# Joined edits on a one-core transformer chain: GpSimd out of most splits and of the state-space mixer, 512-column products with a fold

## The chip, the cores and the metric

The kernel runs on one NeuronCore of a Trainium2 chip. The metric is the device time of one execution in microseconds. Five engines work side by side, each through its own instructions in their order: TensorE (PE, with its weight loads as PEld), VectorE (DVE), ScalarE (ACT), GpSimd (POOL) and SyncE (SP, which here only issues DMAs).

## The reference

A chain of two blocks over one sequence of 256 tokens with 1024 features, all in fp32:

```python
def first_block(x, ...):
    for layer in range(2):
        h = rms_norm(x, norm_mix[layer])
        if layer < 1:
            x = x + s5_mixer(h, ...)                       # state-space mixer, gated output
        else:
            x = x + stick_breaking_attention(h, w_q, k_shared, v_shared, w_o)
        x = x + conv_ffn(rms_norm(x, norm_ffn[layer]), w_up, conv_w, conv_b, w_down)
        if layer == 0:
            kv = rms_norm(x, norm_kv) @ kv_w               # shared keys and values
    return rms_norm(x, norm_final)

def second_block(x, ...):
    for i in range(2):
        x = layernorm(DN_ALPHA * x + 0.5 * swiglu(x, w13[i, 0], w2[i, 0]), ...)
        y = hybrid_mixer(x, ...)    # w_in: windows' q, k, v; conv'd qkv; z; gates
        x = layernorm(DN_ALPHA * x + y, ...)
        x = layernorm(DN_ALPHA * x + 0.5 * swiglu(x, w13[i, 1], w2[i, 1]), ...)
    return x

def s5_mixer(h, ...):
    u = h @ w_in        # then 64 groups of 16 channels, 64 complex states each
    ...                 # bu = u * B, scan with ab = exp(a dt), y = Re(C s) + d u
    z = gelu(y) @ w_glu
    return z[..., :1024] * sigmoid(z[..., 1024:])

def hybrid_mixer(x, ...):
    ...                 # ya: sliding windows of 128, yb: gated delta rule, chunks of 64
    return (sigmoid(gate_a) * (ya @ w_branch_a) + sigmoid(gate_b) * (yb @ w_branch_b)) @ w_out
```

The inner width of the feed-forward networks (FFNs) is 2816; there are two with a convolution of width 3 before the SiLU and four without.

## The kernel before, in words

**Products.** TensorE multiplies in the type fp32r, and each operand is held as a high and a low half: `split` (L146) lets ScalarE cast the operand to its high half (L150) and VectorE subtract that from it for the low half (L154). Its argument `share` gives the last columns of the subtraction to GpSimd. `mm3` (L183) makes one product of three matmuls: high times low, high times high, low times high. `unit` (L158) loads 128 x 1024 weights (512 KB) through the SP queue (L161) into `raw` and splits them into `wh` and `wl`. `cols_steps` (L199) multiplies a unit with the activations: 8 k-tiles of 128 features, each `mm3` over 256 columns, the tokens, all in one PSUM half bank. `toks` and `rows` are the products whose stationary operand is the activations; their matmuls have 256 and 512 columns.

**Order.** TensorE's order is fixed by `weave`, which takes steps from generators by a clock of its own; the other engines' instructions are put in order by the scheduler of the framework. `ahead` loads and splits the first units of the next stage early.

**Stages.** The state-space mixer `ssm` makes, for each of 8 `kt`, `u = w_in h` (`inputs`, unit split with `SH_I` = 384 columns on GpSimd), then builds 128-row matrices from the powers of the decay: `gt` from `Z` and `b`, `ca` from `W` and `c` (`group`), each a complex product: a VectorE multiply, a GpSimd multiply into `prod`, and an add (L770), which is GpSimd's for `ca` from the second `kt` on. The powers in `W` are made by GpSimd too (`step`). Then come scans on VectorE (L819) and 16- to 32-column products. `Glu` follows, with units split with `SH_Y` = 640 columns on GpSimd. In `ffn` (L405) step m of 22 multiplies the gate and the up unit into the two halves of one PSUM bank; `gate` reads the gate half from PSUM (ScalarE's SiLU, L386, or the convolution, L396 to L401), VectorE multiplies with the up half (L423), the result is split (`gh`, `gl`), and the down product of step m - `LAG` (7) follows, accumulated in four banks of the eight. `stick_breaking` has keys, queries and values of the same form; `hybrid` has the windows' keys and queries (`plain`), convolved channels (`conv`, `SH_C`), `z`, gates and branches (`SH_G`, `SH_B`, `SH_Z` = 640). The branches end in sums `keep`, and w_out is a `row_gemm` over 8 units, of which the last MH = 5 go to the hold pools, opened before the spare pool at the end of the kernel's `build`.

Of the kernel before, what the change touches and what calls it, by code (L numbers as in the profile page):

```python
# [12 lines left out]
ALU = mybir.AluOpType  # L13
# [77 lines left out]
class Core:  # L91
# [114 lines left out]

    def toks(self, out, ws, x, t):
# [14 lines left out]
    def ahead(self, x, srcs):  # L222
# [161 lines left out]
    def silu_gate(self, pool, ps, m):  # L384
        s = pool.tile([P, T], F32, name="s")
        self.nc.scalar.activation(out=s, in_=ps[:, 0, :], func=AF.Silu)  # L386
        return s

    def conv_gate(self, cw, cb):
# [3 lines left out]
        def gate(pool, ps, m):  # L393
            g = ps[:, 0, :]
# [11 lines left out]
    def ffn(self, x, state, up, down, gate, tail, after):  # L406
# [5 lines left out]
        with ExitStack() as ctx:  # L412
# [7 lines left out]
            def gated(m, ps):  # L420
                s = gate(act, ps, m)
                p = act.tile([P, T], F32, name="p")
                nc.vector.tensor_tensor(out=p, in0=s, in1=ps[:, 1, :], op=ALU.mult)  # L423
# [11 lines left out]
            def turn():  # L435
                yield "first"
                yield HOP
                for m in range(2):
# [34 lines left out]
SHARE = 512  # L473
# [27 lines left out]
def ssm(c, yT, after):  # L501
# [27 lines left out]
    with ExitStack() as ctx:  # L529
# [27 lines left out]
        with ExitStack() as prep:  # L557
# [111 lines left out]
            def step(R, src, dst, n, l, e=V):  # L669
# [3 lines left out]
                tt(ta, R[:, :, src], l[:, None, 0:1].to_broadcast(sh_), ALU.mult, e)  # L673
                tt(tb, R[:, ::-1, src], l[:, 1:3, None].to_broadcast(sh_), ALU.mult, e)
                tt(R[:, :, dst], ta, tb, ALU.add, e)
# [47 lines left out]
        hx = c.ktiles(hT)  # L723
# [30 lines left out]
        def group(kt):  # L754
# [7 lines left out]
            for R, n, x, y, pool, name in ((Z, TS, "b_re", "b_im", q3, "gt"), (W, TS + 1, "c_re", "c_im", cq, "ca")):  # L762
# [6 lines left out]
                tt(p, f(1), h(y), ALU.mult, G)  # L769
# [1097 lines left out]
```

## Time and profile before

| what | us |
| --- | --- |
| median of three runs (2253.45 to 2261.68) | 2254.35 |
| the profiled execution | 2259.23 |
| its span in the trace | 2257.5 |
| TensorE busy (95%) | 2146.6 |
| weight loads busy (87%) | 1968.0 |
| VectorE busy (65%) | 1466.2 |
| ScalarE busy (49%) | 1102.8 |
| GpSimd busy (23%) | 510.7 |

The span runs from the first to the last instruction in the trace; the execution's time is 1.7 us longer. A matmul's record lasts longer than its share of the engine, since matmuls overlap: the pace of TensorE is read from the distance of the starts. Along the span the stages are: state-space mixer to about 166 us, Glu to 250, convolution FFN to 440, attention to 580, two FFNs to 950, hybrid mixer to 1305, two FFNs to 1690, hybrid mixer to 2052, the last FFN to the end.

### The profile page before, as it was taken

Reading aid. Unit: us, or ns where it says so; the run is one execution under the profiler, and the core shown is the slowest. Engines: PE = TensorE matmul, PEld = TensorE weight load, DVE = VectorE, ACT = ScalarE, POOL = GpSimd, SP = SyncE. Lnnn points to the kernel's source line nnn. Section 1 sums busy time; section 2 is a strip of 40 time slices with the busy share of each in tenths; the row PEclk is TensorE's granted clock in tenths of the full one; section 3 lists DMA queues with packets and bytes.
Section 4 is the critical chain, followed back from the end, with each engine's and each line's share of the span. In section 5 each row is a group of like instructions: output and inputs, shape, how many; then the busy total and the mean of one; then the engine's idle time right before and its main releaser. Section 6 shows DMA issues by size and latency. Waiting matters only on the chain.

```text
span 2257.5 us, 40264 instructions
## 1 busy us (share of the span) xinstructions
PE 2146.6 (95%) x15892; PEld 1968.0 (87%) x15892; DVE 1466.2 (65%) x2352; ACT 1102.8 (49%) x1951; POOL 510.7 (23%) x519
## 2 busy tenths in 40 slices
PE   5679999999999999998999899999999899999998
PEld 5568999888999999897889899989989788998997
DVE  8974766676666555689754765565558886466555
ACT  4344554454545544466555444444445656543442
POOL 7542100101000100252534410020015344342000
PEclk8779999999999999999999999999999999999999
DMA  4214576544556556554443655556565454264663
GB/s 153 66 34 149 167 240 188 173 138 140 177 185 197 183 185 187 165 170 145 133 118 121 207 157 186 185 183 197 186 188 157 133 154 122 92 203 154 194 188 121
DMA packets 123486, 362.27 MB, mean 160 GB/s; under 512 B 24732, under 2 KB 38000, under 8 KB 123296
## 3 DMA queue, kind: packets, MB, share of 16 engines
q1 hardware_dynamic: 117696, 350.25, 49.7%
q0 software_dynamic: 5232, 9.37, 1.5%
q8 instruction: 125, 2.05, 0.4%
q14 instruction: 65, 0.53, 0.1%
q10 hardware_dynamic: 368, 0.07, 0.0%
HBM read 355.36 MB, written 5.04 MB: 160 GB/s over the span
## 4 chain that ended last, share of the span: by engine, by line
PE 75%; DVE 10%; DMA 5%; issue 5%; ACT 2%; POOL 1%; ACTq 0%; POOLq 0%; DVEq 0%
PE ps L36 72%; PE ps L40 3%; DVE wl L154 3%; DMA raw<-in_ffn_w_dram 2%; ACT wh L150 2%; DMA raw<-in_w_in_z_dram 1%; DVE xl L154 1%; DMA k<-scratch 1%; DVE keep L1053 1%; DVE k L1053 1%; DVE ea L513 0%; POOL u L1052 0%; DVE keep L1052 0%; DMA raw<-in_w_out_dram 0%; DVE er L709 0%
## 5 line engine op out<-in xcount | busy, mean ns | idle before, releaser
L154 DVE TENSOR_TENSOR wl<-raw,wh 128x1024 fp32r<-128x1024 f32 (+3 forms) x622 | 718.3, 1158 | 543.4 <-ACT wh L150 541.2
L150 ACT CAST wh<-raw 128x1024 fp32r<-128x1024 f32 x622 | 649.4, 1049 | 659.4 <-PE ps L36 344.2
L36 PE MATMUL ps<-xl,wh 128*128 128x256 f32 x3056 | 880.4, 288 | 8.5 <-DVE xl L154 6.2
L36 PE MATMUL ps<-xh,wh 128*128 128x256 f32 x3056 | 866.1, 283 | 0.0
L36 PE MATMUL ps<-xh,wl 128*128 128x256 f32 x3056 | 865.9, 283 | 0.0
L36 PEld LDWEIGHTS ps<-xl,wh 128*128 128x128 f32 x3056 | 587.9, 192 | 32.8 <-issue 19.1
L36 PEld LDWEIGHTS ps<-xh,wh 128*128 128x128 f32 x3056 | 587.2, 192 | 3.9
L36 PEld LDWEIGHTS ps<-xh,wl 128*128 128x128 f32 x3056 | 586.8, 192 | 0.0
L154 POOL TENSOR_TENSOR wl<-raw,wh 128x512 fp32r<-128x512 f32 (+2 forms) x172 | 293.3, 1709 | 1183.9 <-ACT wh L150 1126.7
L36 PE MATMUL ps<-wl,gh 128*128 128x512 f32 x528 | 208.9, 396 | 0.0
L36 PE MATMUL ps<-wh,gl 128*128 128x512 f32 x528 | 208.3, 394 | 0.5 <-DVE gl L154 0.5
L36 PE MATMUL ps<-wh,gh 128*128 128x512 f32 x528 | 208.0, 394 | 0.0
L36 PE MATMUL ps<-wl,xh 128*128 128x256 f32 (+1 forms) x576 | 188.2, 327 | 11.8 <-DVE wl L154 11.8
L36 PE MATMUL ps<-wh,xl 128*128 128x256 f32 (+1 forms) x576 | 183.1, 318 | 0.8 <-DVE xl L154 0.7
L36 PE MATMUL ps<-wh,xh 128*128 128x256 f32 (+1 forms) x576 | 182.4, 317 | 0.0
L36 PEld LDWEIGHTS ps<-wl,xh 128*128 128x128 f32 x576 | 110.7, 192 | 21.4 <-DVE wl L154 12.7
L36 PEld LDWEIGHTS ps<-wh,gl 128*128 128x128 f32 x528 | 99.2, 188 | 24.3 <-DVE gl L154 1.3
L36 PEld LDWEIGHTS ps<-wh,xl 128*128 128x128 f32 x576 | 110.8, 192 | 9.9 <-DVE xl L154 2.7
L36 PEld LDWEIGHTS ps<-wh,xh 128*128 128x128 f32 x576 | 111.0, 193 | 6.5
L36 PEld LDWEIGHTS ps<-wl,gh 128*128 128x128 f32 x528 | 99.7, 189 | 18.8
L36 PEld LDWEIGHTS ps<-wh,gh 128*128 128x128 f32 x528 | 99.2, 188 | 18.5
L150 ACT CAST xh<-ps 128x512 fp32r<-128x512 f32 (+1 forms) x68 | 34.0, 517 | 115.5 <-PE ps L40 113.3
(286 smaller groups left out, 2446.8 us busy)
## 6 DMA issues: line engine op xcount, KB each, us to landing
raw<-in_ffn_w_dram SPq DMA_DIRECT2D x264, 512.0 KB, 4.3
raw<-in_ffn_w_up_dram SPq DMA_DIRECT2D x88, 512.0 KB, 4.1
raw<-in_w_in_qkv_dram SPq DMA_DIRECT2D x48, 512.0 KB, 4.1
raw<-in_ffn_w_down_dram SPq DMA_DIRECT2D x44, 512.0 KB, 3.9
raw<-in_w_in_gate_dram SPq DMA_DIRECT2D x32, 512.0 KB, 3.6
raw<-in_w_branch_dram SPq DMA_DIRECT2D x32, 512.0 KB, 3.6
raw<-in_ssm_w_glu_dram SPq DMA_DIRECT2D x16, 512.0 KB, 3.5
raw<-in_w_in_z_dram SPq DMA_DIRECT2D x16, 512.0 KB, 3.6
```

Source lines behind the costliest of these rows:

```text
L36: self.pe.matmul(out, lhsT=lhsT, rhs=rhs, start=start, stop=stop)
L40: self.pe.transpose(out, in_, ident)
L150: o = [self.nc.scalar.copy(out=h, in_=src).ins]
L154: r = e.tensor_tensor(out=l[..., c], in0=src[..., c], in1=h.bitcast(F32)[..., c], op=ALU.subtract)
L1053: stt = lambda o, a, s, b, op0, op1, e=V: e.scalar_tensor_tensor(out=o, in0=a, scalar=s, in1=b, op0=op0, op1=op1)
```

## The change

It joins several edits.

1. `wide_steps` replaces `cols_steps` for the up products of the FFNs, the shared keys, the queries, the windows' keys and queries, the gates and the branches, 340 units in all. The activations' halves lie side by side in one tile, so that one 512-column matmul multiplies the high weights with both, and a 256-column one the low weights with the high activations: 16 matmuls and weight loads for a unit, where there were 24. The result is in two halves of a PSUM bank; `fold` adds them: a ScalarE copy of the one into SBUF, a VectorE instruction that adds the other. The FFN's gate and up products have a bank each, and gate and multiply read the folded tiles.
2. GpSimd leaves every split but those of the 48 convolved units (512 columns): 80 splits of 640 columns, 36 of 512 and 8 of 384 are VectorE's whole.
3. In the state-space mixer GpSimd's multiplies, adds and `W` steps go to VectorE, and the input product is made in plain fp32: w_in and the normed input are not split, 64 matmuls of 256 columns where there were 192.
4. At the end of the hybrid mixers the spare pool is opened before the hold pools.

Over the program TensorE's instructions (matmuls and transposes) go from 14772 to 11924, VectorE's from 2354 to 2717, ScalarE's from 1840 to 2140, GpSimd's from 524 to 365.

```diff
+    def wide_steps(self, out, w, x):
+        both = out.rearrange("p a b -> p (a b)")
+        for k in range(KD):
+            a = slice(k * P, (k + 1) * P)
+            high = lambda: self.pe.matmul(both, lhsT=w[0][:, a], rhs=x[k][2].rearrange("p a b -> p (a b)"),
+                                          start=k == 0, stop=k == KD - 1)
+            if k < KD - 1:
+                high()
+            self.pe.matmul(out[:, 1], lhsT=w[1][:, a], rhs=x[k][0], start=False, stop=False)
+            if k == KD - 1:
+                high()
+            if k % 3 == 2:
+                yield 1
+
+    def fold(self, s, ps, scale=1.0):
+        self.nc.scalar.activation(out=s, in_=ps[:, 1], func=AF.Copy, scale=scale)
+        self.nc.vector.scalar_tensor_tensor(out=s, in0=ps[:, 0], scalar=scale, in1=s, op0=ALU.mult, op1=ALU.add)
+        return s
...
-                ws.append([self.unit(src[j], SHARE, stay=True) for j in range(2)])
+                ws.append([self.unit(src[j], stay=True) for j in range(2)])
...
-        return tuple(self.hp[i].tile([P, KD, T], F32R, name=f"x{s}") for s in "hl")
+        both = self.hp[i].tile([P, KD, 2, T], F32R, name="xx")
+        return both[:, :, 0], both[:, :, 1], both
...
                     if m < MF:
-                        ps = self.ps(2, T)
                         for c in range(2):
-                            yield from self.cols_steps(ps[:, c, :], self.unit(up[m - 2, c]), self.ktiles(x))
-                        gated(m, ps)
+                            ps = self.ps(2, T)
+                            yield from self.wide_steps(ps, self.unit(up[m - 2, c]), self.ktiles(x))
+                            if c == 0:
+                                s = gate(act, self.fold(act.tile([P, T], F32, name="sum"), ps), m)
+                        u = self.fold(act.tile([P, T], F32, name="sum"), ps)
+                        gated(m, s, u, u)
...
-                step(W, slice(0, n), slice(n, 2 * n), n, l, G if WP_[0] else V)
-            step(W, slice(4, 5), slice(8, 9), 1, l4, G if WP_[0] else V)
+                step(W, slice(0, n), slice(n, 2 * n), n, l)
+            step(W, slice(4, 5), slice(8, 9), 1, l4)
...
-            w = c.unit(I["ssm_w_in"][kt], SH_I)
+            w = c.raw.tile([P, 1024], F32, name="raw")
+            nc.sync.dma_start(out=w, in_=I["ssm_w_in"][kt])
             pu = c.ps(T)
-            yield from c.cols_steps(pu, w, hx)
+            for k in range(KD):
+                PE.matmul(pu, lhsT=w[:, k * P:(k + 1) * P], rhs=hT[:, k, :], start=k == 0, stop=k == KD - 1)
+                if k % 2:
+                    yield 1
...
-                tt(p, f(1), h(y), ALU.mult, G)
-                add = (G if R is W and kt >= GADD else V).tensor_tensor(out=o, in0=o, in1=p, op=ALU.add).ins
-                last = last if R is W and kt >= GADD else add
+                tt(p, f(1), h(y), ALU.mult)
+                last = V.tensor_tensor(out=o, in0=o, in1=p, op=ALU.add).ins
...
         def query(m):
-            w = c.unit(I["attn_w_q"][m], SH_S)
-            pq = c.ps(T)
-            yield from c.cols_steps(pq, w, xq)
-            qs[m] = wk.tile([P, T], F32, name="qT")
-            S.activation(out=qs[m], in_=pq, func=AF.Copy, scale=0.125)
+            w = c.unit(I["attn_w_q"][m])
+            pq = c.ps(2, T)
+            yield from c.wide_steps(pq, w, xq)
+            qs[m] = c.fold(wk.tile([P, T], F32, name="qT"), pq, 0.125)
...
-                w = c.unit(W("gate")[side * KD + m], SH_G)
-                p = c.ps(T)
-                yield from c.cols_steps(p, w, hx)
+                w = c.unit(W("gate")[side * KD + m])
+                p = c.ps(2, T)
+                yield from c.wide_steps(p, w, hx)
                 dst[m] = keep1(T)
-                c.act(out=dst[m], in_=p, func=AF.Tanh, scale=0.5)
+                c.fold(dst[m], p)
+                c.act(out=dst[m], in_=dst[m], func=AF.Tanh, scale=0.5)
...
             if kind == "mix":
+                c.spare_pool(cn)
                 c.hold_pools(cn, MH, MR)
-                c.spare_pool(cn)
```

Keys, `plain` and branches change as the queries do. Where the instructions stand now, at three places:

VectorE in the state-space mixer, where `gt` and `ca` of the first groups are made, before (`ea`, `eb` belong to the tables for the scan):

```order
L513 TENSOR_TENSOR gt<-Z,b_re 128x1024 x2
L513 TENSOR_TENSOR ca<-W,c_re 128x1152 x2
L154 TENSOR_TENSOR wl<-raw,wh 128x640
L770 TENSOR_TENSOR gt<-gt,prod 128x1024
L770 TENSOR_TENSOR ca<-ca,prod 128x1152
L513 TENSOR_TENSOR ea<-count,turnh 128x512
L513 TENSOR_TENSOR eb<-count,turnl 128x512
L513 TENSOR_TENSOR ca<-W,c_re 128x1152
```

and GpSimd beside it:

```order
L513 TENSOR_TENSOR Es<-W,sm_299 128x2x64 x2
L513 TENSOR_TENSOR W<-Es 128x2x64
L513 TENSOR_TENSOR prod<-Z,b_im 128x8x128
L513 TENSOR_TENSOR prod<-W,c_im 128x1152
L154 TENSOR_TENSOR wl<-raw,wh 128x384
L154 TENSOR_TENSOR wl<-raw,wh 128x640
L513 TENSOR_TENSOR prod<-Z,b_im 128x8x128
L513 TENSOR_TENSOR prod<-W,c_im 128x1152
L154 TENSOR_TENSOR wl<-raw,wh 128x640
L770 TENSOR_TENSOR ca<-ca,prod 128x1152
```

VectorE there now:

```order
L529 TENSOR_TENSOR gt<-Z,b_re 128x1024
L529 TENSOR_TENSOR prod<-Z,b_im 128x8x128
L529 TENSOR_TENSOR prod<-W,c_im 128x1152
L529 TENSOR_TENSOR gt<-Z,b_re 128x1024
L795 TENSOR_TENSOR gt<-gt,prod 128x1024
L795 TENSOR_TENSOR ca<-ca,prod 128x1152
L529 TENSOR_TENSOR ea<-count,turnh 128x512
L529 TENSOR_TENSOR eb<-count,turnl 128x512
L529 TENSOR_TENSOR prod<-Z,b_im 128x8x128
L529 TENSOR_TENSOR prod<-W,c_im 128x1152
L529 TENSOR_TENSOR er<-ea,eb 128x512
L795 TENSOR_TENSOR gt<-gt,prod 128x1024
```

GpSimd's multiplies stand between VectorE's own, and the low half of w_in is gone.

VectorE in an FFN of the second block, one step of m before (`p` is the gated result, `gl` its low half):

```order
L423 TENSOR_TENSOR p<-s,ps 128x256
L154 TENSOR_TENSOR wl<-raw,wh 128x1024
L154 TENSOR_TENSOR gl<-p,gh 128x256
L154 TENSOR_TENSOR wl<-raw,wh 128x1024 x2
L423 TENSOR_TENSOR p<-s,ps 128x256
```

and now (`sum` is a folded tile):

```order
L154 TENSOR_TENSOR gl<-sum,gh 128x256
L154 TENSOR_TENSOR wl<-raw,wh 128x1024
L225 SCALAR_TENSOR_TENSOR sum<-ps,sum 128x256
L154 TENSOR_TENSOR wl<-raw,wh 128x1024
L225 SCALAR_TENSOR_TENSOR sum<-ps,sum 128x256
L442 TENSOR_TENSOR sum<-s,sum 128x256
L154 TENSOR_TENSOR wl<-raw,wh 128x1024
L154 TENSOR_TENSOR gl<-sum,gh 128x256
```

A step has two folds more, each behind a low half of weights; no other instruction is added.

SyncE at the end of the first hybrid mixer, before (`in_w_out` is w_out, `in_ffn_w` the next FFN's weights):

```order
L161 DMA raw<-in_w_out_dram 128x1024 x2
L161 DMA raw<-in_w_branch_dram 128x1024 x7
L161 DMA raw<-in_w_out_dram 128x1024 x2
L161 DMA raw<-in_w_branch_dram 128x1024 x2
L161 DMA raw<-in_w_out_dram 128x1024
L161 DMA raw<-in_w_branch_dram 128x1024
L161 DMA raw<-in_w_out_dram 128x1024 x3
L161 DMA raw<-in_ffn_w_2_0_dram 128x1024 x3
L303 DMA gain<-in_ln_g_dram 128x1024
L303 DMA gain<-in_ln_b_dram 128x1024
```

and now:

```order
L161 DMA raw<-in_w_branch_dram 128x1024 x9
L161 DMA raw<-in_w_out_dram 128x1024 x2
L161 DMA raw<-in_w_branch_dram 128x1024 x7
L161 DMA raw<-in_w_out_dram 128x1024 x3
L161 DMA raw<-in_ffn_w_2_0_dram 128x1024 x4
L161 DMA raw<-in_ffn_w_2_dram 128x1024
L324 DMA gain<-in_ln_g_dram 128x1024
L324 DMA gain<-in_ln_b_dram 128x1024
L161 DMA raw<-in_w_out_dram 128x1024 x2
L161 DMA raw<-in_ffn_w_2_dram 128x1024 x2
L161 DMA raw<-in_w_out_dram 128x1024
```

Five w_out units stood among the branches' loads and three behind them; now two stand among them and three behind them, and the last three stand after units of the next FFN and behind the gains.

## Rows read from the trace of the kernel before

**Rows 1.** The page: span, then busy time of each engine.

```profile
span 2257.5 us, 40264 instructions
...
PE 2146.6 (95%) x15892; PEld 1968.0 (87%) x15892; DVE 1466.2 (65%) x2352; ACT 1102.8 (49%) x1951; POOL 510.7 (23%) x519
```

**Rows 2.** Windows: stretch, length; busy us of PE, PEld, DVE, ACT, POOL; PEclk, DMA, GB/s.

```profile
0.00:166.00 166.00, 109.67 (x760) 93.25 (x761) 147.31 (x186) 71.23 (x131) 95.94 (x83) 0.80 0.32 86
...
950.00:1125.00 175.00, 164.58 (x1304) 147.51 (x1301) 146.33 (x305) 107.45 (x225) 78.29 (x101) 0.97 0.49 150
...
1305.00:1690.00 385.00, 382.19 (x2701) 357.50 (x2700) 217.17 (x269) 172.76 (x234) 25.78 (x19) 1.00 0.60 186
```

**Rows 3.** Lines by form, 0 to 170 us, VectorE, then GpSimd: busy us, mean ns, idle before.

```profile
L513 DVE TENSOR_TENSOR ca<-W,c_re 128x1152 f32<-128x1152 f32 x8 | 16.9, 2126 | 11.5 <-PE ps L36 11.5
...
L513 DVE TENSOR_TENSOR gt<-Z,b_re 128x1024 f32<-128x1024 f32 x8 | 13.5, 1702 | 0.0
...
L709 DVE TENSOR_SCALAR er<-er 128x512 f32<-128x512 f32 x4 | 9.4, 2358 | 0.0
...
L513 POOL TENSOR_TENSOR prod<-W,c_im 128x1152 f32<-128x1152 f32 x8 | 20.6, 2572 | 7.2 <-DVE gt L770 7.0
...
L513 POOL TENSOR_TENSOR prod<-Z,b_im 128x1024 f32<-128x1024 f32 x8 | 19.5, 2434 | 30.7 <-DVE gt L770 26.5 <-DVE Z L513 4.2
...
L770 POOL TENSOR_TENSOR ca<-ca,prod 128x1152 f32<-128x1152 f32 x6 | 17.3, 2886 | 19.2 <-DVE ca L513 19.2
```

**Rows 4.** Timeline, 84.5 to 113 us: start, duration, instruction.

```profile
84.69 2.70 POOL L513 TENSOR_TENSOR prod<-W,c_im 128x1152 f32<-128x1152 f32 x1
...
85.31 2.36 DVE L709 TENSOR_SCALAR er<-er 128x512 f32<-128x512 f32 x1
...
87.93 0.41 DVE L710 TENSOR_SCALAR er<-er 128x512 f32<-128x512 f32 x1
...
111.06 1.36 DVE L513 TENSOR_TENSOR ca<-W,c_re 128x1152 f32<-128x1152 f32 x1 [2.12 <-PE ps L36]
```

**Rows 5.** Lines by form, whole span: low halves of weights, and kin of the fold's instructions.

```profile
L154 DVE TENSOR_TENSOR wl<-raw,wh 128x1024 fp32r<-128x1024 f32 x450 | 551.6, 1229 | 457.4 <-ACT wh L150 456.4
...
L154 DVE TENSOR_TENSOR wl<-raw,wh 128x384 fp32r<-128x384 f32 x80 | 79.8, 997 | 45.6 <-ACT wh L150 45.4
...
L154 DVE TENSOR_TENSOR wl<-raw,wh 128x512 fp32r<-128x512 f32 x84 | 78.7, 939 | 40.4 <-ACT wh L150 39.4 <-PE ps L36 0.5 <-PE ps L40 0.2
...
L386 ACT ACTIVATE s<-ps 128x256 f32<-128x256 f32 x88 | 33.2, 378 | 0.0
...
L1053 DVE SCALAR_TENSOR_TENSOR keep<-keep,ps 128x256 f32<-128x256 f32 x32 | 13.2, 413 | 8.5 <-PE ps L36 8.5
```

**Rows 6.** Timeline of TensorE: plain fp32 matmuls, two records each.

```profile
109.99 0.38 PE L36 MATMUL ps<-M,U 128*32 128x128 f32 x2
...
110.21 0.38 PE L36 MATMUL ps<-ca,Sx 128*32 128x128 f32 x2
```

**Rows 7.** Timeline of TensorE: FFN products (256, 512, 256 columns), then w_out's.

```profile
2152.79 0.28 PE L36 MATMUL ps<-xl,wh 128*128 128x256 f32 x1
...
2158.48 0.40 PE L36 MATMUL ps<-wl,gh 128*128 128x512 f32 x1
...
2161.28 0.28 PE L36 MATMUL ps<-xl,wh 128*128 128x256 f32 x1
...
2167.02 0.40 PE L36 MATMUL ps<-wl,gh 128*128 128x512 f32 x1
...
1283.21 0.39 PE L36 MATMUL ps<-wl,xh 128*128 128x512 f32 x1
...
1284.34 0.39 PE L36 MATMUL ps<-wh,xl 128*128 128x512 f32 x1
```

**Rows 8.** TensorE's waits after 166 us; windows at the first w_out.

```profile
PE ps L36 <- DVE wl L154: 12.1, 3, 6.3
...
1284.70:1287.50 2.80, 0.03 (x1) 0.00 (x0) 2.35 (x5) 1.35 (x2) 1.26 (x2) 0.99 0.54 157
...
1287.50:1294.30 6.80, 3.32 (x8) 2.64 (x9) 3.99 (x3) 1.99 (x2) 2.17 (x2) 0.50 0.72 227
```

More of the change, by code (lines that the diff above doesn't have):

```diff
@@ L381, in arrive, with silu_gate @@
         self.done.add(f"in{t}")
-    def silu_gate(self, pool, ps, m):
+    def silu_gate(self, pool, g, m):
         s = pool.tile([P, T], F32, name="s")
-        self.nc.scalar.activation(out=s, in_=ps[:, 0, :], func=AF.Silu)
+        self.nc.scalar.activation(out=s, in_=g, func=AF.Silu)
         return s
@@ L418, in ffn, with gated @@
             self.done.discard("first")
[L420 to L423, printed above, removed]
+            def gated(m, s, u, p):
+                nc.vector.tensor_tensor(out=p, in0=s, in1=u, op=ALU.mult)
                 gts[m] = tuple(gp.tile([P, T], F32R, name=f"g{i}") for i in "hl")
@@ L442, in turn @@
                             self.pe.transpose(ps[:, c, t * P:(t + 1) * P], state[c][:, t, m * P:(m + 1) * P], self.ident)
-                    gated(m, ps)
+                    gated(m, gate(act, ps[:, 0, :], m), ps[:, 1, :], act.tile([P, T], F32, name="sum"))
             def main():
@@ L472 @@
 LAG = 7
-SHARE = 512
 HOLD = 6
@@ L603, in ssm @@
                 G.memset(turn[:, 1:], 0.5 * np.pi)
-            hT = c.pair(0)
+            hT = one.tile([P, KD, T], F32, name="hT")
             for t in range(2):
-                c.flip(hT, c.rms(t, c.rms_stat(t), g, c.x[:, t, :]), t)
+                xn = c.rms(t, c.rms_stat(t), g, c.x[:, t, :])
+                for q in range(2):
+                    ps = c.ps(4, P)
+                    for j in range(4):
+                        k = q * 4 + j
+                        PE.transpose(ps[:, j, :], xn[:, k * P:(k + 1) * P], c.ident)
+                    S.copy(out=hT[:, q * 4:q * 4 + 4, t * P:(t + 1) * P], in_=ps)
             with c.tc.issue_after(c.power):
@@ L667, in ssm, with step @@
                    for v in (Er, Es) for n in range(2)]
[L669 removed]
+            def step(R, src, dst, n, l):
                 sh_ = [P, 2, n, NG]
                 ta, tb = (v[:, :, :n] for v in (tmp[:2] if R is Z else tmp[2:]))
[L673 to L675 removed]
+                tt(ta, R[:, :, src], l[:, None, 0:1].to_broadcast(sh_), ALU.mult)
+                tt(tb, R[:, ::-1, src], l[:, 1:3, None].to_broadcast(sh_), ALU.mult)
+                tt(R[:, :, dst], ta, tb, ALU.add)
             l2 = square(l1)
@@ L934, in keys @@
         def keys(m):
-            w = c.unit(I["kv_w_k"][m], SH_S)
-            pk = c.ps(T)
-            yield from c.cols_steps(pk, w, xk)
-            S.copy(out=kT[:, m, :], in_=pk)
+            w = c.unit(I["kv_w_k"][m])
+            pk = c.ps(2, T)
+            yield from c.wide_steps(pk, w, xk)
+            c.fold(kT[:, m, :], pk)
         def turn():
@@ L1164, in plain @@
         def plain(src, dst, scale):
-            w = c.unit(src, SH_QA)
-            p = c.ps(T)
-            yield from c.cols_steps(p, w, hx)
-            S.activation(out=dst, in_=p, func=AF.Copy, scale=scale)
+            w = c.unit(src)
+            p = c.ps(2, T)
+            yield from c.wide_steps(p, w, hx)
+            c.fold(dst, p, scale)
         def qkv_a():
@@ L1174, in qkv_a @@
             p = c.ps(2, T)
-            yield from c.toks256_steps(p, W("va")[0], hT, SH_QA)
+            yield from c.toks256_steps(p, W("va")[0], hT)
             ka["v"] = keep2(2, T)
@@ L1189, in z_gate @@
             p = c.ps(2, T)
-            yield from c.toks256_steps(p, W("z")[n], hT, SH_Z)
+            yield from c.toks256_steps(p, W("z")[n], hT)
             z_done(n, p)
```

39 lines of the change are left out of this document (14 added, 25 removed).

## The prediction

> **What bounds the kernel now.** First the page [rows 1]: TensorE is busy 95% of a span of 2257.5 us, its weight loads 87%, VectorE 65%, GpSimd 23%. An average hides stages, so next the windows [rows 2]. In 0 to 166 us, the state-space mixer, it is the other way round: VectorE 147.31 of 166 us (89%), GpSimd 95.94, TensorE 109.67 at a granted clock of 0.80; TensorE idles 56 us there. From then on it hardly stops: 2257 - 166 = 2091 us hold 2146.6 - 109.7 = 2036.9 us of it, and in 1305 to 1690 (two FFNs) 382.19 of 385. So a gain must come from VectorE in the first 166 us, and from fewer or quicker matmuls after them; work taken off GpSimd or VectorE later is worth nothing by itself.
>
> **Mixer, GpSimd's work to VectorE.** The view by line and shape [rows 3] shows VectorE slow there: `ca<-W,c_re` takes 2126 ns in the mean, the same instruction with GpSimd idle 1.36 us [rows 4]; `er` at L709 takes 2358 ns, the equal-sized L710 0.41. The timeline shows why: L709 starts at 85.31 inside GpSimd's `prod<-W,c_im` (84.69, 2.70 us), ends as that ends, and has lost 1.95 us, 72% of GpSimd's time. GpSimd is busy 95.94 us [rows 2], 57.4 of them prods and `ca` adds [rows 3]; if between a half and 72% of that is lost to VectorE, 48 to 69 us of VectorE's 147 are waiting inside instructions. I take 60, which is also what the 186 instructions give when each is charged against the shortest of its kind. All of it should go, since what GpSimd keeps there are memsets and one-column operations.
>
> What VectorE gets, at undisturbed durations (1.36 us for 1152 columns, so 1.21 for 1024): 8 prods of 1024 columns, 9.7; 8 of 1152, 10.9; 7 `ca` adds, 9.5; 12 steps of `W`, of up to 512 columns, at L710's 0.41 us, 5; 5 Glu splits widened from 384 to 1024 columns, by 0.23 us each [rows 5] or, undisturbed and by their columns, some 0.7, so 1 to 3.5, say 3. What it loses: the low halves of `w_in` and `hT`, 8 of 640 columns and 4 of 512, 9 us. Net -60 + 38 - 9 = -31 us, bounds -19 and -40.
>
> TensorE's input product changes from 192 fp32r matmuls (192 x 0.1185 = 23 us) to 64 plain ones. A plain 128-column matmul is two records; pairs start 0.22 us apart at full clock [rows 6], so 256 columns take 0.43 and 64 of them 28 us, 5 more, and about 14 more if the clock is at its lower level then. TensorE has 56 idle us to put this in, but `U` waits for it. Of VectorE's 31 I take 24; bounds 10 and 40.
>
> **Wide products.** 340 units of 8 k-tiles, 2720 k-tiles, lose one weight load and merge two 256-column matmuls into one of 512. The columns stay the same. In an FFN [rows 7] 48 matmuls of 256 run from 2152.79 to 2158.48, 118.5 ns each, 12 of 512 to 2161.28, 233.3 each, and the next 48 to 2167.02, 119.6 each. So a merge saves 2 x 118.5 - 233.3 = 3.7 to 2 x 119.6 - 233.3 = 5.9 ns: 10 to 16 us; I take 12. The fastest 512-column products, in w_out, start 1.13 us apart over five, 226 ns: then 11 ns a merge, 30 us, the upper end; the lower is 0. The Trainium skill ("TensorE: Matmul & The Clock Gate", section "Back-to-back issue gap") gives an isolated matmul N/2.4 + 2.5 ns at full clock, and says that this counts no weight load. By that a merge would save 2.5 ns and the sum would have 7 us here in place of 12; the rows put the saving above it.
>
> **Folds.** Each product adds an ACT copy of one PSUM half and a VectorE add of the other; nearest rows: 378 ns and 413 ns [rows 5]. In an FFN 240 x 0.41 = 99 us of VectorE (16 us in an FFN's 190, on top of some 56%) are hidden: VectorE has 168 us idle in the 385 of 1305 to 1690, the PSUM bank of a fold is wanted again only four products (8 us) later, and the gated result first 7 steps later (`LAG`). If that cover went, they would be on the path. Each up product takes a bank of its own, two for a step where one served, of the four the accumulators leave. In attention and mixer the fold of a query sits ahead of the scores that read it: one ACT, one VectorE instruction, behind at most one 1.23 us split, against one ACT before. Eight queries and as many `qa` at 0.25 us on the path: +4; bounds 0 and +16.
>
> **Splits outside the mixer.** 80 low halves grow from 384 to 1024 columns on VectorE, 0.997 to 1.229 us, 36 from 512, 0.939 to 1.229 [rows 5]; a narrow one was dear because of GpSimd beside it, so these cost 29 us in all and take the slow-down of their neighbours with them. Beside a TensorE that is busy: 0. Their cover is VectorE's idle time, 28.7 of 175 us in its fullest stretch, 950 to 1125 [rows 2].
>
> **Tail of the mixers.** The w_out weights are loaded in another order on the SP queue: the held units 3 to 7 were partly among the branch weights, now three stand ahead of five FFN units and the rest after them. Today TensorE waits 6.3 us there for one low half [rows 8] (12.1 in three waits in all), and the granted clock, 0.99 in the 2.8 us before, in which TensorE ran only 0.03, is 0.50 in 1287.5 to 1294.3, the lower level of 1.2 GHz. New: units 0 to 2 give 36 products of 512 columns, 8.4 us, and the last loads come later, with two raw buffers; by hand the waits sum to some 6 us again. I take 0; bounds -6 (gone in both mixers, less what follows) and +12.
>
> **Sum.** -24 - 12 + 0 + 4 = -32 against the profiled execution (2259.2): 2227. The median of the runs, 2254.35, lies 4.9 lower, so 2222.
>
> **Rivals** (times against the median).
> 1. *The mixer hands the bound to TensorE.* Its clock was 0.80, its inputs are now dearer by up to 14, and the chain at each `kt` is one after the other; then VectorE's 31 are worth 10 and the sum is -10 - 12 + 4: 2236. For it: TensorE's clock there; against: TensorE busy 110 of 166.
> 2. *Wide products bring nothing,* as the columns are the same and weight loads already run beside matmuls: -24 + 4: 2234. For it: 118.5 is close to half of 233.3. Or the opposite, the weight loads (87% busy) are the brake and a third fewer let 512 columns run at 226: -24 - 30 + 4: 2204. The Trainium skill ("Perfetto Trace Analysis", section "Identifying the Most-Contended Engine") would judge TensorE by the busy share of its weight loads rather than of its matmuls; the row of 233.3 ns, almost two of 118.5 with one load in place of two, speaks against the loads as the brake.
> 3. *Slower: VectorE becomes the bound in mixers and attention.* There 100 folds (41 us) and 116 larger splits (29 us) come in front of what TensorE waits for, in one queue, with `k`, `keep` and `xl` behind them. It decides from the point where a stretch's idle VectorE is used up: 28.7 us in 950 to 1125, against some 6 us of folds and 6 of splits there. If all 70 lay on the path: -24 - 12 + 70 on 2254: 2288. Against: GpSimd's disturbance, 78.29 us in that stretch, goes.
> 4. *Nothing moves:* mixer -10 by its lower bound, wide products 0, tails and folds +8: 2252.
>
> **How the numbers follow.** 0.5% (11 us) is about what a measurement of this kernel can tell from no change: faster is below 2243, slower above 2265.6. Chances: forecast 0.45, rival 1 0.13, rival 2 0.10 without gain and 0.13 with weight loads as the brake, rival 4 0.11, rival 3 0.08. Faster holds the forecast, rival 1 and both halves of rival 2, together 0.81, of which 0.01 goes to terms that miss together: 0.80; same, rival 4 with that 0.01, 0.12; slower, rival 3, 0.08. Range: from 2188 (mixer -40, pace -30, folds +4: -66) to 2250, which leaves out rival 3 and most of rival 4.
>
> **What would show it.** Right: in 0 to 140 us of the changed kernel VectorE's `ca<-W,c_re` and `prod` near 1.36 us, GpSimd almost empty; the switch to Glu some 24 us earlier; in an FFN one 512-column and one 256-column matmul in about 352 ns per k-tile (now 356); TensorE's idle after the mixer near 50 us. Wrong: `prod` above 1.6 us on VectorE with GpSimd idle (the slow-down had another cause); TensorE at half clock through the first stretch; VectorE named as releaser of TensorE for over 20 us in a mixer stretch; FFN steps longer than before, with `wl` or `sum` as releaser.

## The result, and the profile after

The changed kernel takes 2225.34 us in the median of its runs, against 2256.64 for the kernel before: 0.9861 of it, with a 95% interval of 0.9837 to 0.9884. That is 31.3 us less. The forecast was 32 less, 2222, and the range 2188 to 2250.

The page of the changed kernel answers to [rows 1]:

```profile
span 2226.1 us, 35096 instructions
...
PE 2133.7 (96%) x13108; PEld 1824.4 (82%) x13108; DVE 1570.7 (71%) x2715; ACT 1200.0 (54%) x2251; POOL 228.8 (10%) x360
```

TensorE is busy 12.9 us less in a span 31.4 us shorter, VectorE 104 us more, GpSimd 282 us less.

Its windows answer to [rows 2] (the same columns: stretch, length, busy us of PE, PEld, DVE, ACT, POOL, then the granted clock, DMA share, GB/s):

```profile
0.00:142.00 142.00, 114.80 (x758) 97.07 (x758) 118.17 (x217) 72.56 (x133) 7.34 (x33) 0.90 0.36 100
...
920.00:1097.00 177.00, 167.56 (x1254) 144.99 (x1253) 149.44 (x331) 109.06 (x234) 76.63 (x110) 0.98 0.49 154
...
1276.00:1661.00 385.00, 380.17 (x2065) 326.61 (x2064) 258.67 (x350) 199.51 (x314) 10.83 (x12) 1.00 0.57 183
```

The first stretch, some 24 us shorter, has GpSimd at 7 us and VectorE at 118; TensorE's granted clock is 0.90 in the mean of its two levels, where it was 0.80. In its fullest mixer stretch VectorE keeps 27.6 us idle, and in the FFNs 126 of 385.

VectorE's lines by form in the first 150 us answer to [rows 3]:

```profile
L529 DVE TENSOR_TENSOR ca<-W,c_re 128x1152 f32<-128x1152 f32 x8 | 10.7, 1352 | 3.0 <-PE ps L36 2.9
...
L529 DVE TENSOR_TENSOR prod<-W,c_im 128x1152 f32<-128x1152 f32 x8 | 10.8, 1350 | 0.0
...
L529 DVE TENSOR_TENSOR prod<-Z,b_im 128x1024 f32<-128x1024 f32 x8 | 9.7, 1216 | 0.0
...
L731 DVE TENSOR_SCALAR er<-er 128x512 f32<-128x512 f32 x4 | 1.7, 417 | 0.0
```

`ca<-W,c_re` fell from 2126 ns to 1352, `er` from 2358 to 417: with GpSimd silent each instruction takes its undisturbed time.

In the timeline of TensorE, in the same FFN as [rows 7], a k-tile is now one matmul of 512 and one of 256 columns:

```profile
2147.88 0.39 PE L36 MATMUL ps<-xx,wh 128*128 128x512 f32 x1
...
2148.11 0.28 PE L36 MATMUL ps<-xx,wl 128*128 128x256 f32 x1
...
2149.64 0.40 PE L36 MATMUL ps<-xx,wh 128*128 128x512 f32 x1
```

Five k-tiles in 1.76 us are 352 ns each, where three matmuls of 118.5 made 356.

TensorE's waits after the state-space mixer answer to [rows 8]:

```profile
PE ps L36 <- DVE wl L154: 21.6, 8, 6.4
```

The wait for low halves of weights rose from 12.1 us to 21.6; 19.2 of it lie at the two w_out products.

### The profile page after: what moved, and what is told of

Same layout as the page of the kernel before. It is cut to its first block, busy times and chain, and to the rows that moved or that the text cites. A ratio compares the mean times of both kernels' runs of the same rounds, so it can differ in the third digit from the quotient of the medians.

```text
span 2226.1 us, 35096 instructions
## 1 busy us (share of the span) xinstructions
PE 2133.7 (96%) x13108; PEld 1824.4 (82%) x13108; DVE 1570.7 (71%) x2715; ACT 1200.0 (54%) x2251; POOL 228.8 (10%) x360
## 4 chain that ended last, share of the span: by engine, by line
PE 73%; DVE 8%; DMA 8%; issue 4%; ACT 3%; POOL 1%; SPq 0%; POOLq 0%; DVEq 0%; ACTq 0%
PE ps L36 70%; PE ps L40 3%; DVE wl L154 3%; ACT wh L150 2%; DMA raw<-in_ffn_w_dram 2%; DMA raw<-in_w_out_dram 1%; DMA raw<-in_ssm_w_glu_dram 1%; DMA raw<-in_w_in_z_dram 1%; DMA raw<-in_ffn_w_down_dram 1%; DMA k<-scratch 1%; DVE prod L529 1%; DVE keep L1073 0%; DMA raw<-in_kv_w_v_dram 0%; POOL u L1072 0%; DVE k L1073 0%
## 5 line engine op out<-in xcount | busy, mean ns | idle before, releaser
L36 PE MATMUL ps<-xx,wh 128*128 128x512 f32 (+1 forms) x3392 | 1067.6, 374 | 4.9 <-DVE xx L154 3.0
L154 DVE TENSOR_TENSOR wl<-raw,wh 128x1024 fp32r<-128x1024 f32 (+1 forms) x614 | 736.8, 1202 | 285.3 <-ACT wh L150 275.9
L36 PE MATMUL ps<-xx,wl 128*128 128x256 f32 x2992 | 788.2, 281 | 0.2 <-DVE wl L154 0.2
L36 PEld LDWEIGHTS ps<-xx,wh 128*128 128x128 f32 x3392 | 599.4, 190 | 111.1 <-issue 18.2
L36 PEld LDWEIGHTS ps<-xx,wl 128*128 128x128 f32 x2992 | 567.2, 190 | 28.4 <-DVE wl L154 0.5
L36 PE MATMUL ps<-wh,xx 128*128 128x256 f32 (+1 forms) x1152 | 259.5, 320 | 0.8 <-DVE xx L154 0.7
L36 PE MATMUL ps<-wl,xx 128*128 128x256 f32 (+1 forms) x576 | 190.9, 331 | 22.1 <-DVE wl L154 21.4
L36 PEld LDWEIGHTS ps<-wh,xx 128*128 128x128 f32 x1152 | 194.4, 194 | 16.7 <-DVE xx L154 3.0
L225 DVE SCALAR_TENSOR_TENSOR sum<-ps,sum 128x256 f32<-128x256 f32 x240 | 101.2, 423 | 114.3 <-ACT sum L224 114.2
L36 PEld LDWEIGHTS ps<-wl,xx 128*128 128x128 f32 x576 | 111.6, 194 | 36.0 <-DVE wl L154 26.3
L36 PEld LDWEIGHTS ps<-wh,gl 128*128 128x128 f32 x528 | 99.3, 188 | 24.8 <-DVE gl L154 1.6
```

Source lines behind the costliest of these rows:

```text
L36: self.pe.matmul(out, lhsT=lhsT, rhs=rhs, start=start, stop=stop)
L154: r = e.tensor_tensor(out=l[..., c], in0=src[..., c], in1=h.bitcast(F32)[..., c], op=ALU.subtract)
L225: self.nc.vector.scalar_tensor_tensor(out=s, in0=ps[:, 0], scalar=scale, in1=s, op0=ALU.mult, op1=ALU.add)
```

## The experiments

Twelve kernels were run. To read them, the span of each is cut at the same events: the start of the first down product of the first FFN ("to FFN 1": the state-space mixer, Glu and seven steps of the FFN), and for each hybrid mixer the time from the last down product of the FFN ahead to the first of the FFN behind, without TensorE's waits at w_out. These waits are the times between two starts of w_out's matmuls beyond 0.23 us, where they exceed 0.9. All of it is read from the starts of TensorE's instructions in one traced execution of each kernel; the medians are of all its runs, and a traced execution lay up to 6 us from its kernel's median (e1's was the fastest of twelve). The kernel before, run again beside the experiments, had medians of 2256.85 (e1 to e4), 2258.71 (l1 to l4) and 2258.2 (f1 to g3), so a difference of 2 us between these sets tells nothing.

```
kernel                       median  to FFN 1  mixer 1, 2    waits at w_out  six FFNs
before                       2256.6   290.1    407.4 409.4    6.4   5.7       961.6
after                        2225.3   263.9    405.1 404.6    9.3   9.9       955.1
e1 mixer's edits alone       2251.0   265.8    407.5 406.5   12.3  13.4       960.6
e2 wide products alone       2269.2   284.7    409.1 408.4   14.4  15.7       956.9
e3 splits alone              2244.0   287.1    403.4 403.1    6.4   4.5       964.7
e4 pools' order alone        2267.7   285.9    409.9 408.1   10.9   9.9       962.7
l1 all but mixer's edits     2255.8   286.3    404.6 406.5   14.0  14.1       956.7
l2 all but wide products     2232.0   266.3    405.4 403.8   10.9   9.4       962.1
l3 all but splits            2242.4   263.8    411.1 410.4   14.1  12.6       952.8
l4 all but pools' order      2222.6   264.3    403.3 401.9    9.9   9.9       955.3
f1 w_out loaded first        2225.6   265.8    405.2 408.5    6.0   6.9       955.9
g1 GpSimd work in mixer      2250.1   289.0    404.0 403.0    9.1   9.1       954.8
g2 fp32r input product       2231.4   261.3    404.5 405.6   13.7  14.3       955.0
g3 GpSimd work in hybrids    2245.7   263.4    407.4 407.7   13.1  14.2       957.7
```

Six FFNs sums four stretches: from the first to the last down product of FFN 1, from the first of FFN 2 to the last of FFN 3, the same of 4 and 5, and from the first of FFN 6 to the end. The stretch of the attention, 174 to 180 us in all of them, stands in no column.

### One part at a time

e1 gives the state-space mixer its edits and nothing else:

```diff
-                step(W, slice(0, n), slice(n, 2 * n), n, l, G if WP_[0] else V)
+                step(W, slice(0, n), slice(n, 2 * n), n, l)
...
-                tt(p, f(1), h(y), ALU.mult, G)
+                tt(p, f(1), h(y), ALU.mult)
...
+                PE.matmul(pu, lhsT=w[:, k * P:(k + 1) * P], rhs=hT[:, k, :], start=k == 0, stop=k == KD - 1)
```

> The kernel before with the edits of the state-space mixer alone (GpSimd's multiplies, adds and W steps on VectorE, plain fp32 input product). Theory (VectorE, slowed by GpSimd beside it, sets the mixer's time): about 25 us faster than the kernel before, 20 to 30, nearly all of the whole change, and the first FFN's down products start 24 to 28 us earlier than at 290.1. Rival (the gain is GpSimd's disturbance in the whole program, or the pace of TensorE): 10 us or less.

It was 0.9977 (0.9964 to 0.9991) of the kernel before, 5.8 us faster: by the total a miss. But the first down product started at 265.8, 24 us earlier, as the theory had it. In the trace 13.6 us of that are lost again at w_out, where TensorE now waited up to 13.3 us at once; the traced execution was 14 us faster than the one before, so why the median gained only 5.8 is not shown in full:

```profile
PE ps L36 <- DVE wl L154: 28.1, 6, 13.3
...
0.00:142.00 142.00, 111.13 (x723) 94.38 (x724) 118.80 (x213) 67.59 (x126) 16.92 (x38) 0.88 0.37 100
```

e2 has the wide products and the folds alone, with GpSimd's shares:

```diff
                 w = c.unit(W("gate")[side * KD + m], SH_G)
-                p = c.ps(T)
-                yield from c.cols_steps(p, w, hx)
+                p = c.ps(2, T)
+                yield from c.wide_steps(p, w, hx)
...
+                c.fold(dst[m], p)
```

> The kernel before with the 512-column products and folds alone, GpSimd's shares as they were. Theory (a merge saves 4 to 6 ns, folds hidden): 5 to 12 us faster, each FFN's down stretch about 1.5 us shorter. Rival one (columns are the same, nothing is saved): within 3 us. Rival two (folds on a VectorE that GpSimd still disturbs come on the path): slower by 5 us or more, TensorE waiting for folded tiles.

1.0064 (1.004 to 1.0088), 12 us slower, so the number fell to rival two, but not for its reason: the FFNs are 4.7 us shorter, no folded tile is among the large waits, and w_out again waits 18 us longer than before, for weights:

```profile
PE ps L36 <- DVE wl L154: 29.4, 4, 11.3
```

e3 takes GpSimd out of the splits alone:

```diff
-SHARE = 512
+SHARE = 0
-SH_Y = 640
+SH_Y = 0
-SH_G = SH_B = SH_Z = 640
+SH_G = SH_B = SH_Z = 0
```

> The kernel before with GpSimd out of the splits of Glu, z, gates, branches and of the first units of a stage, nothing else. Theory (TensorE is busy there, so neither VectorE's relief nor its 29 us of extra work matters): within 4 us of the kernel before. Rival (the disturbance by GpSimd costs time there too): 8 us faster or more. Other rival (larger low halves come late): 5 us slower or more.

0.9949 (0.9933 to 0.9966), 13 us faster: the theory fell, the rival stands. The windows of the first hybrid mixer, before and in e3:

```profile
950.00:1280.00 330.00, 318.34 (x2714) 292.18 (x2712) 236.25 (x525) 190.96 (x442) 147.72 (x165) 0.98 0.47 145
```

```profile
945.00:1275.00 330.00, 320.30 (x2740) 294.23 (x2740) 239.70 (x532) 191.69 (x444) 87.00 (x130) 0.99 0.47 146
...
PE ps L36 <- DVE wl L154: 10.7, 2, 6.3
```

GpSimd has 61 us less to do in the same 330 us, and TensorE gets 2 us more done; each of the two mixers is 4 to 6 us shorter, without its wait at w_out.

Part of this can be placed. TensorE's waits for `k` in the two mixers sum to 9.7 and 10.3 us before and to 7.9 and 7.6 in e3; those for `keep` are 1.7 in all four. One of them, in the first mixer before and then in e3:

```profile
PE ps L40 <- ACT k L252: 2.4, 1, 2.4
```

```profile
PE ps L40 <- ACT k L252: 1.3, 2, 1.1
```

So 1.8 of 4.0 us and 2.7 of 6.3 are shorter waits for `k`.

e4 swaps the two pools and nothing else:

```diff
+                c.spare_pool(cn)
                 c.hold_pools(cn, MH, MR)
-                c.spare_pool(cn)
```

> The kernel before with the spare pool opened before the hold pools at the end of the mixers, nothing else. The prediction had 0 for it. By the trace of the changed kernel, where TensorE stands 6.1 + 3.3 us at w_out in the first mixer and 6.5 + 3.4 in the second against 6.4 and 5.7 before, it costs 3 us a mixer: 4 to 8 us slower. Rival (the second wait comes from the splits' larger halves, not from the order): within 2 us.

1.0058 (1.0035 to 1.0082), 11 us slower: the way that was expected, but more than the 4 to 8. The waits are 10.9 and 9.9 for 6.4 and 5.7, 8.7 us in all. TensorE's and GpSimd's orders are those of the kernel before.

Alone, then, the four parts give -5.8, +12.3, -12.9 and +10.8, together +4, and joined they give -31. The column of the waits tells most of why: alone they lengthen the waits at w_out by 13.6, 18.0, -1.2 and 8.7 us, together 39, joined by 7. These 32 us cannot be set straight against the 36 by which the sum of the medians is off, since they come from one execution each: the traced executions alone sum to -12, against -31 joined, which is 20 off. There the waits make 32 the one way, and the first stretch gives 11 back, since the traced 290.1 of the kernel before is 3 to 5 us above the other kernels without the mixer's edits.

### All but one part

l1 to l4 are the changed kernel with one part as it was before; each edit is the reverse of one above.

> The changed kernel with the state-space mixer as before (GpSimd back in its multiplies, adds, W steps and splits; fp32r input product). Theory (the mixer's part is worth 21 to 24 us whatever stands behind it, as the first FFN's down products show): 2246 to 2250, first down product at 284 to 288. Rival (parts depend on each other, since alone the edit gave only 6 us): 2231 or less.

2255.84, 0.9993 (0.9983 to 1.0002) of the kernel before: 30 more than the changed kernel, and more than the theory's total. The first down product starts at 286.3, 22 us later, as expected; the other 9 are longer waits at w_out.

> The changed kernel with products of 256 columns and no folds. Theory (a merge saves some 6 ns in every FFN, 1.5 us for each FFN and little elsewhere): 2231 to 2235. Rival (wide products cost, as the run of them alone was 12 us slower): 2222 or faster.

2232.0, as expected: 6.7 more. The intervals, 0.9872 to 0.9904 here and 0.9837 to 0.9884 for the changed kernel, overlap; what speaks for the 6.7 is the trace, where the six FFNs take 7.0 more.

> The changed kernel with GpSimd back in the splits of Glu, z, gates, branches and first units. Theory (GpSimd beside VectorE costs 4 us in the body of each mixer, as the run of the splits alone showed, against 0 in the prediction): 2232 to 2237. Rival (that run's gain came from another place of w_out's loads, not from the splits): within 4 us of 2225.

2242.39, 0.9934 (0.9922 to 0.9946) and 17 more than the changed kernel, more than expected: the mixers take 6 us more each, the waits at w_out 7.5, at the changed kernel's order of loads, and all waits for low halves rise to 27.8 us:

```profile
PE ps L36 <- DVE wl L154: 27.8, 9, 5.9
```

> The changed kernel with the hold pools opened first again. Theory (the order of the pools fixes TensorE's waits at w_out to 9.5 us a mixer, where the old order leaves them to the scheduler, 6 in the kernel before and 12 to 13 in the run of the mixer's edits alone): waits of 6 or of 12 and more for both mixers, so 2218 or 2230 and more, and nothing else moves. Rival (the waits at w_out do not set the end): within 2 us of 2225.

2222.63, 0.984 (0.9828 to 0.9853), beside 0.9861 (0.9837 to 0.9884) for the changed kernel: no difference that the intervals tell. The waits were 9.9 in both mixers; neither 6 nor 12, so the theory of a choice between two was wrong, and the rival is nearer. In this company the pools' order is worth nothing.

### What GpSimd's work costs VectorE

g1 lets GpSimd do each `prod` once more, into a tile that nothing reads; the orders of VectorE, ScalarE and SyncE are the changed kernel's.

```diff
                 tt(p, f(1), h(y), ALU.mult)
+                tt(extra[:, :, :n], f(1), h(y), ALU.mult, G)
```

> The changed kernel with 16 multiplies of 1024 and 1152 columns for GpSimd beside VectorE's own in the state-space mixer, into a tile that nothing reads; the other engines' orders are the same. Theory (GpSimd's work stretches VectorE's instructions, and VectorE sets the stage): GpSimd about 40 us busy there, VectorE 20 to 29 us longer in the same instructions, first down product 12 to 25 us later than 263.9, in all 2236 to 2250. Rival (the gain came from a shorter chain without a hand-over between the two engines, or from the plain input product): within 5 us of 2225.

2250.11: 24.8 us more than the changed kernel, by work that no one waits for, and the first down product at 289.0, 25 us later and where the kernel before had it; both at the upper end of what was expected. Its lines by form, and its first window:

```profile
L797 DVE TENSOR_TENSOR ca<-ca,prod 128x1152 f32<-128x1152 f32 x8 | 16.3, 2035 | 0.0
...
L529 POOL TENSOR_TENSOR extra<-Z,b_im 128x1024 f32<-128x1024 f32 x8 | 25.7, 3216 | 56.7 <-DMA b_im<-in_ssm_b_im_dram 39.1 <-DMA raw<-in_ssm_w_in_dram 17.4
...
L529 POOL TENSOR_TENSOR extra<-W,c_im 128x1152 f32<-128x1152 f32 x8 | 23.1, 2890 | 8.6 <-DMA c_im<-in_ssm_c_im_dram 8.1
...
0.00:142.00 142.00, 100.73 (x603) 83.36 (x603) 131.32 (x192) 61.83 (x112) 56.27 (x49) 0.84 0.35 98
```

Summed over its instructions, VectorE spends 31 us beyond the shortest duration of each kind in 0 to 150 us, where the changed kernel spends 1.6 (in 0 to 142). Compared one by one with the changed kernel's first stretch, 16 of VectorE's 217 instructions are longer, by 1.3 to 2.1 us, and every other by 0.01 us at most: one for each of GpSimd's 16 multiplies. The timeline shows how:

```profile
29.16 1.23 DVE L529 TENSOR_TENSOR gt<-Z,b_re 128x1024 f32<-128x1024 f32 x1
...
29.29 2.98 POOL L529 TENSOR_TENSOR extra<-Z,b_im 128x1024 f32<-128x1024 f32 x1 [17.37 <-DMA raw<-in_ssm_w_in_dram]
...
30.30 3.05 DVE L529 TENSOR_TENSOR prod<-Z,b_im 128x1024 f32<-128x1024 f32 x1
...
32.35 3.12 POOL L529 TENSOR_TENSOR extra<-W,c_im 128x1152 f32<-128x1152 f32 x1
...
33.28 3.40 DVE L529 TENSOR_TENSOR prod<-W,c_im 128x1152 f32<-128x1152 f32 x1
...
35.55 3.02 POOL L529 TENSOR_TENSOR extra<-Z,b_im 128x1024 f32<-128x1024 f32 x1
...
36.61 3.04 DVE L529 TENSOR_TENSOR gt<-Z,b_re 128x1024 f32<-128x1024 f32 x1
```

GpSimd's 2.98 starts while VectorE's 1.23 runs; VectorE's next starts at 30.30, and ends at 33.35, 1.08 us after GpSimd's end at 32.27. GpSimd's next ends at 35.47, 2.12 after that, and VectorE's next at 36.68, 1.21 after that: the two take turns, whole instructions at a time. Undisturbed, these two of VectorE's take 1.22 us (1024 columns) and 1.35 (1152), 0.14 more than the 1.08 and 1.21 between the ends. VectorE's 31 us over the 16 multiplies are 1.9 us each, near the 2.12 that GpSimd has between VectorE's end and its own; GpSimd's own records, 48.8 us in all, are longer because they hold its waiting too. The Trainium skill says so of the port pair that the two engines share ("SBUF — State Buffer", section "SBUF: two separate sides"): an instruction of VectorE with two SBUF inputs and one of GpSimd that reads SBUF exclude each other for its whole length, whoever is second being blocked. By that rule an instruction of GpSimd costs a busy VectorE its own length, and this trace agrees with it: 1.9 us for 2.1.

g2 makes the mixer's input product in fp32r again, with both halves made on ScalarE and VectorE:

```diff
-            w = c.raw.tile([P, 1024], F32, name="raw")
-            nc.sync.dma_start(out=w, in_=I["ssm_w_in"][kt])
+            w = c.unit(I["ssm_w_in"][kt])
             pu = c.ps(T)
+            yield from c.cols_steps(pu, w, c.ktiles(hT))
```

> The changed kernel with the mixer's input product in fp32r again, both halves made by ScalarE and VectorE alone. Theory (VectorE sets the stage): 8 low halves of 1.22 us and 4 of 0.68 more on VectorE, 5 us less on TensorE: first down product 5 to 12 us later, in all 2230 to 2237. Rival (plain fp32 costs TensorE as much as it saves VectorE): within 3 us of 2225.

2231.35, in the theory's range, and the theory is wrong: the first down product came 2.6 us earlier, not later, though VectorE has 7.8 us more to do in the window. The total is not clear of the changed kernel's (0.9866 to 0.9897 beside 0.9837 to 0.9884). In the trace the waits at w_out are 8.8 us longer, and the timeline shows them begin with seven units of the FFN ahead of w_out's last on the SP queue, where the changed kernel has five:

```profile
0.00:142.00 142.00, 106.06 (x788) 93.88 (x789) 125.93 (x222) 75.94 (x134) 8.94 (x36) 0.88 0.37 100
...
1240.00 14.02 SPq L161 DMA_DIRECT2D raw<-in_ffn_w_dram  x7
```

g3 adds a subtraction for GpSimd to each split of gates and branches, with the other engines' orders as they were, but for a swap or two on VectorE:

```diff
+        if extra:
+            self.nc.gpsimd.tensor_tensor(out=self.extra, in0=raw[:, 384:], in1=raw[:, :640], op=ALU.subtract)
```

> The changed kernel with a 640-column subtraction for GpSimd beside each split of gates and branches, 32 a mixer, into a tile that nothing reads; the other engines' orders are the same but for a swap or two. Theory (GpSimd beside VectorE is what the mixers paid for in the kernel before): mixers without the waits at w_out 3 to 6 us longer each, those waits up to 4 more each: 2233 to 2243. Rival (the splits' hand-over to GpSimd, not its work, was the cost): within 4 us of 2225.

2245.7, 20 more (0.9934 to 0.996, clear of 0.9837 to 0.9884) and above the theory's 2243. In the trace the two mixers take 2.3 and 3.1 more and the waits at w_out 3.8 and 4.3, 13.5 in all. The traced execution was the fastest of its six, 12.7 us above the changed kernel's, so these 13.5 are all that it has to place; where the other executions lost more no trace shows. For scale: g1, whose mixers are the changed kernel's, differs from it there by 1.1 and 1.6 us. The windows and two lines by form, here and in the changed kernel:

```profile
915.00:1245.00 330.00, 318.33 (x2402) 275.26 (x2401) 257.94 (x558) 193.62 (x463) 147.41 (x163) 0.99 0.44 138
...
L155 DVE TENSOR_TENSOR wl<-raw,wh 128x1024 fp32r<-128x1024 f32 x50 | 68.1, 1363 | 5.9 <-ACT wh L151 5.7
...
L169 POOL TENSOR_TENSOR extra<-raw 128x640 f32<-128x640 f32 x32 | 55.2, 1726 | 70.8 <-DMA raw<-in_w_in_gate_dram 36.0 <-DMA raw<-in_w_branch_dram 33.1 <-DMA k<-scratch 1.3
```

```profile
915.00:1245.00 330.00, 320.56 (x2417) 277.71 (x2416) 252.17 (x570) 197.17 (x471) 89.37 (x131) 0.99 0.46 143
...
L154 DVE TENSOR_TENSOR wl<-raw,wh 128x1024 fp32r<-128x1024 f32 x52 | 63.5, 1222 | 8.3 <-ACT wh L150 7.8
```

58 us more on GpSimd lengthen VectorE's low halves from 1222 to 1363 ns and cost TensorE 2.2 us of work in the stretch.

### The waits at w_out

In the changed kernel the timeline of SyncE and TensorE at the first w_out reads:

```profile
1231.15 5.97 SPq L161 DMA_DIRECT2D raw<-in_w_out_dram  x3
...
1238.27 10.96 SPq L161 DMA_DIRECT2D raw<-in_ffn_w_dram  x5
...
1261.30 0.80 PE L36 MATMUL ps<-wl,xx 128*128 128x512 f32 x1 [5.90 <-DVE wl L154]
...
1267.09 0.79 PE L36 MATMUL ps<-wl,xx 128*128 128x512 f32 x1 [2.86 <-DVE wl L154]
```

SyncE spends 10.96 us in issuing five units of the next FFN, waiting for buffers, and w_out's last three stand behind them; TensorE waits twice. The granted clock, here in two windows, is then at its lower level (0.50, 1.2 GHz) for the products that follow the second wait, after a stretch in which TensorE ran 3.90 us of 12.70; the six products between the two waits already start some 0.43 us apart, where 0.23 is usual:

```profile
1254.40:1267.10 12.70, 3.90 (x10) 2.16 (x10) 5.92 (x5) 3.56 (x4) 0.00 (x0) 0.68 0.66 253
...
1267.10:1271.40 4.30, 4.30 (x10) 3.43 (x11) 1.39 (x2) 0.00 (x0) 0.00 (x0) 0.50 0.75 222
```

f1 puts the FFN's first loads behind w_out's, but leaves the gains ahead of w_out's last three:

```diff
+            with (self.tc.issue_after(self.sent) if self.late else ExitStack()):
+                self.early()
```

> The changed kernel with the next FFN's first loads put behind all of w_out's on the SP queue at the end of the mixers. Theory (TensorE waits at w_out because its last three units are loaded behind five units of the FFN, for whose buffers the queue waits): the waits of 9.3 and 9.9 us fall below 5, some 10 us in all: 2213 to 2219. Rival (the memory of the hold pools comes free late, or the FFN's units are then late): waits of 9 as before or moved behind the norm: 2222 to 2230.

2225.64, the same as the changed kernel, as the rival had it. The waits fell from 19.2 to 12.9 us, so their cause is shown in part, but the 6 us did not reach the end; TensorE waits longer for the norm's `x` behind w_out, 9.0 us where it had 6.4:

```profile
PE ps L36 <- DVE wl L155: 15.8, 7, 3.5
...
PE ps L40 <- DVE x L394: 9.0, 5, 2.2
```

The rest was not placed. On the SP queue the gains' load now stood where the FFN's units had stood, and w_out's last three were issued from 1250.89 us on, only 2.4 us earlier than in the changed kernel:

```profile
1248.59 0.33 SPq L326 DMA_DIRECT2D gain<-in_ln_g_dram  x1
...
1250.89 6.86 SPq L162 DMA_DIRECT2D raw<-in_w_out_dram  x3
```

So f1 did not try w_out's loads with nothing ahead of them. Over all the traces the order of the loads goes with the waits only in part. With all of w_out ahead of the FFN's units the kernel before and e3 wait 12.1 and 10.9 us, but e1, whose order of loads at w_out is that of the kernel before, 25.7. With seven units ahead, l1 and g2 wait 28.1 and 28.0. At the changed kernel's order, l2 and g1 wait 20.3 and 18.2, like the changed kernel (19.2), but l3 and g3, with more of GpSimd's work in the mixers, 26.7 and 27.3. What sets the waits beside the order was not taken apart. No version was found that is faster than the changed kernel beyond the intervals.

## Why the prediction was right

The gain was met within a microsecond (31.3 for 32; the time, 2225.34 for 2222, within 3.3). That is luck in part: the mixer's term came nearly as forecast, and the others were off by amounts that cancel.

- **The mixer: -24, found -22.** The first down product starts at 264.8 in the mean of the seven kernels that have all of these edits and no extra work in the stage (263.4 to 266.3), and at 286.8 in the five without. The mechanism is shown by g1: 49 us of GpSimd's records, for work that nothing reads, give all of it back. What was wrong inside the term is the input product. The prediction counted VectorE's 9 us of saved low halves as part of the gain and 5 us on TensorE against it; by g2 the plain product gains nothing here. Nor do its rows give the 14 us that it set for a lower clock: at half the clock 64 products of 0.43 us would take 28 us more (an estimate). The 60 us inside VectorE's instructions were right in size, and all but a few went.
- **Wide products: -12, found -7 in the FFNs.** l2 is 6.7 us slower than the changed kernel. The pace came as read, 352 ns a k-tile, and by 4 ns over 2720 k-tiles that would be 11 us; the FFNs hold 1920 of these, so their 7 us are 3.6 ns each, the lower end of what was read. In the mixers it brought nothing that these runs can tell.
- **Folds: +4, and hidden in the FFNs.** No wait for a folded tile of an FFN shows; their 101 us on VectorE fit its idle time. The +4 in mixers and attention was not measured by itself; the attention's stretch took 176.6 us before, 177.9 in the changed kernel and 177.8 in l2, which has no folds.
- **Splits outside the mixer: 0, found about -9 in the mixers' bodies.** This step failed: "Beside a TensorE that is busy: 0". Without w_out's waits a hybrid mixer takes 408.8 us in the mean of the five kernels with GpSimd in these splits, and 404.5 in that of the eight without and with no idle work there (both mixers together 814 to 822 us, and 805 to 814). In all, the splits are worth 13 us alone (e3) and 17 in the changed kernel (l3), where 7.5 of it lie at w_out. It was the disturbance that the prediction counted for the first stage and left out of the later ones, because VectorE had idle time there. That GpSimd's work by itself costs time there is shown by g3. By e3 somewhat under half of the bodies' part is shorter waits for `k`, none of it waits for `keep`; the rest was not taken apart. Why VectorE's idle time does not help is argued only: it is no use to an instruction that something is waiting for.
- **Tail of the mixers: 0, found +7.** The wait was in the prediction, its size was not. The bounds of -6 to +12 held it. Since the splits' part lies in these waits too, the two terms are not cleanly apart.

One sign that was named for "right" did not come: TensorE's idle time behind the mixer is 65 us, not near 50. It was 54 before; the waits for low halves alone grew by 9.5.

Rival 1 lost: TensorE did not take the mixer over. Of rival 2, neither half came: a merge saves some 4 ns, not 0 and not 11. Rival 3 lost, since VectorE keeps 27.6 us idle in the stretch where it was to run out. Rival 4 lost with them. The range was wide enough for something that the prediction did not know: the waits at w_out ranged from 11 to 30 us over these kernels, moved by edits in other places, in part through the scheduler's order on the SP queue.

## What to carry to other kernels

Elementwise work given to GpSimd beside a VectorE that matters can cost VectorE about the GpSimd instruction's own length, here 1.9 us for a multiply of 1024 or 1152 columns, 64% of GpSimd's busy time in the trace; count it as VectorE's work. Do so where VectorE is the bound, and do not put it at nothing where TensorE is: in the hybrid mixers it cost time too. When parts of a change are tried alone, compare stage by stage and not by the end: here four parts sum to +4 us alone and to -31 joined, and most of the difference is one wait at the end of a stage that three of them were not about. And where loads for the next stage are issued early, look at which queue they stand in, and ahead of what.

## What the runs showed that was not expected

VectorE and GpSimd alternate by whole instructions: in g1 instructions of VectorE with 1.2 to 1.35 us of work took 3.05, 3.40 and 3.04 us. A plain fp32 product in place of an fp32r product of three matmuls, of which the prediction expected a few microseconds either way in the mixer, moved the stage by 2.6 us to the worse in one trace of each, about as much as the traces with the plain product differ among themselves (263.4 to 266.3): it gained nothing.
